# The load phase of a two-layer encoder kernel: squares held behind the splits of x, first weights in pieces, two chunks of x from ScalarE's queue

## The chip, the cores and the metric

The kernel runs on one core of a Trainium2 chip. The metric is the device time of one execution in microseconds; of several runs the median counts. All inputs start in the chip's memory (HBM), and the output ends there. Engines are named as in the profile: PE is TensorE, DVE VectorE, ACT ScalarE, POOL GpSimd, SP SyncE, which here only issues DMAs.

## What is computed

The reference is a trunk of two layers over 512 positions of width 1024, all float32. Each layer adds half of a SwiGLU feed-forward block, an attention mixer, half of a second feed-forward block, and a gated embedding. Cut to what the change touches:

```
h = x
h = h + 0.5 * swiglu(rmsnorm(h, norm_ffn1[0]), w_gate, w_up, w_down)
rmsnorm(x, g) = x * rsqrt(mean(x * x) + 1e-6) * g
swiglu(x)     = (silu(x @ w_gate) * (x @ w_up)) @ w_down
```

The first norm therefore needs the squares of all 1024 features of x, summed for each position. Its factor `rsqrt(...)` is one number for each position, so the kernel multiplies `x * g` by the weights first, and by that factor afterwards.

## The kernel before

**Layout.** The residual `h` is kept transposed, as 8 chunks (c = 0 to 7) of 128 features by 512 positions, 256 KB each. Weights come in units of 128 x 1024 (512 KB), eight 128 x 128 tiles side by side; a unit times the 8 chunks gives one output tile of 128 x 512.

**Three products for one.** To keep float32 accuracy each operand is split into a high part, rounded to the matmul's format, and a low part, the rest. ACT writes the high part (`activation` with Copy, L121 for weights, L168 for x times the gain), DVE the low part (L122 and L169), and PE does three matmuls (`mm3`, L142 high by high, L143 low x by high weights, L144 high x by low weights). One unit is 24 matmuls of 512 columns.

**The load phase.** `setup` loads the gains and the identity matrix from ACT's queue, makes a bfloat16 copy of the identity on DVE (`identb`, L97, read by nothing else in the program), and issues `WARM` = 12 matmuls on zeros (L109) to keep PE busy until data comes. Then it loads x chunk by chunk from SP's queue; after chunk 0 and chunk 2 it loads the first two weight units (`gu1[0, 0, 0]`, the gate, and `gu1[0, 0, 1]`, the up projection), which the first feed-forward tile takes from the list `ahead`. Each chunk is split as it lands (`norm_split`).

**The first norm.** `norm_square` (L175) squares a chunk on ACT; POOL adds the squares of chunks 1 to 7 into the tile `ssq` of chunk 0, seven adds in a row (L180), each of which needs the one before. `stat` then sums over the partitions with four small matmuls against ones on PE (L187, eight passes in the profile), DVE scales the sum (`ms`, L189), POOL takes the power -0.5 (`rcol`, L190), PE spreads the result over the partitions with four transposes (L206), and ACT copies it to `R` (L214). L236 and L238 multiply the finished output tiles by `R`.

**Order.** A tile framework schedules each engine's stream once, ahead of time, from the program's dependences and its own estimate of times; at run time every engine executes its stream in order and waits on semaphores. In the program `ffn` calls the eight `norm_square` behind the first two units (`if m == 0 and i == 0 and which == 1`); the scheduler moves squares forward to where it takes their chunk as landed. `keep_in_program_order`, used by the change, forbids that for one instruction: it stays behind everything traced before it on its engine.

**Buffers.** Raw weights have 3 buffers, high and low parts 4 each, temporaries (the squares of chunks 1 to 7 among them) 8; PE writes output tiles to 3 + 2 banks (`mm`, `sc`), so it can run some units ahead of `R`. Each DMA takes one of 8 semaphore lanes in turn, and a queue waits before it issues a DMA whose lane is still in use.

Of the kernel before, what the change touches and what calls it, by code (L numbers as in the profile page):

```python
# [11 lines left out]
BF16 = mybir.dt.bfloat16  # L12
AF = mybir.ActivationFunctionType
ALU = mybir.AluOpType

P = 128
# [12 lines left out]
UNIT = 8 * P  # L29
N_NORM = 4 * DEPTH + 1  # L30
OPEN = 2
PART = .8
WARM = 12
RPB_W = 48


class Trunk:
# [52 lines left out]
    def setup(self):  # L90
        nc, io = self.nc, self.io
        self.gain = self.cp.tile([P, N_NORM, KC], F32, name="gain")
        nc.scalar.dma_start(self.gain, io["gain"])
        self.ident = self.cp.tile([P, P], F32, name="ident")
        nc.scalar.dma_start(self.ident, io["ident"])
        self.identb = self.cp.tile([P, P], BF16, name="identb")
        nc.vector.tensor_copy(self.identb, self.ident)  # L97
        self.ones = self.cp.tile([P, P], F32, name="ones")
        nc.vector.memset(self.ones, 1.0)
        self.mhalf = self.cp.tile([P, 8], F32, name="mhalf")  # L100
        nc.vector.memset(self.mhalf, -0.5)

        warm = self.small("warm", [P, 1])
        nc.scalar.activation(warm, self.ones[:, 0:1], AF.Silu)
        idle = self.cp.tile([P, T], BF16, name="idle")
        nc.vector.memset(idle, 0.0)
        bank = self.tbank()
        for _ in range(WARM):
            nc.tensor.matmul(bank, idle[:, 0:P], idle, start=True, stop=True)  # L109
        self.h = [None] * KC  # L110
        self.begin_norm(0)
        for c in range(KC):
            self.h[c] = self.hp.tile([P, T], F32, tag="h", name=self.nm("h"))
            nc.sync.dma_start(self.h[c], io["xT"][:, c, :])
            self.norm_split(c)
            if c in (0, 2):
                self.ahead.append(self.unit(io["gu1"][0, 0, c // 2]))


    def split(self, src, hi, lo, lo_eng=None):  # L120
# [5 lines left out]
        self.turn = (self.turn + 1) % 3  # L126
        return self.nc.vector if self.turn else self.nc.gpsimd

    def unit(self, src, cols=UNIT, lo_eng=None):

        nc = self.nc
        raw = self.wr.tile([P, UNIT], F32, tag="wr", name=self.nm("wr"))
        hi = self.wh.tile([P, UNIT], F32R, tag="wh", name=self.nm("wh"))
        lo = self.wl.tile([P, UNIT], F32R, tag="wl", name=self.nm("wl"))
        nc.sync.dma_start(raw[:, :cols], src)
        self.split(raw[:, :cols], hi[:, :cols], lo[:, :cols], lo_eng)
        return hi, lo

    def mm3(self, out, stat, mov, start, stop):
# [32 lines left out]
    def norm_square(self, c):  # L172
        nc = self.nc
        sq = self.tmp() if c else self.small("ssq", [P, T], bufs=1)
        nc.scalar.activation(sq, self.h[c], AF.Square)  # L175
        if c == 0:
            self.acc = sq
        else:
            eng = nc.vector if c == KC - 1 and self.k else nc.gpsimd
            eng.tensor_tensor(self.acc, self.acc, sq, op=ALU.add)  # L180
# [881 lines left out]
```

## Time and profile before

| | us |
|---|---|
| median of 3 runs | 2126.43 |
| the three runs | 2123.27, 2126.43, 2127.14 |
| the profiled execution, its own time | 2126.64 |
| span of its instructions | 2124.8 |
| PE busy | 2085.4 (98%) |
| DVE busy | 1132.3 (53%) |
| ACT busy | 783.8 (37%) |
| POOL busy | 352.3 (17%) |

The span runs from the first to the last instruction; 1.84 us of the execution's time lie outside it. Start times in the rows below are microseconds from the start of the span. An engine's row in a timeline gives start, duration, engine, line, what it writes and reads, how many were merged, and in brackets how long the engine was idle before and what ended that. Durations of neighbours on one engine overlap a little, so the distance from one start to the next is what an instruction costs its engine. PE's granted clock, 1.00 or 0.50 in the rows, is its share of 2.4 GHz; 0.50 is 1.2 GHz.

### The profile page before, as it was taken

Reading aid. Unit: us, or ns where it says so; the run is one execution under the profiler, and the core shown is the slowest. Engines: PE = TensorE matmul, PEld = TensorE weight load, DVE = VectorE, ACT = ScalarE, POOL = GpSimd, SP = SyncE. Lnnn points to the kernel's source line nnn. Section 1 sums busy time; section 2 is a strip of 40 time slices with the busy share of each in tenths; the row PEclk is TensorE's granted clock in tenths of the full one; section 3 lists DMA queues with packets and bytes.
Section 4 is the critical chain, followed back from the end, with each engine's and each line's share of the span. In section 5 each row is a group of like instructions: output and inputs, shape, how many; then the busy total and the mean of one; then the engine's idle time right before and its main releaser. Section 6 shows DMA issues by size and latency. Waiting matters only on the chain.

```text
span 2124.8 us, 25520 instructions
## 1 busy us (share of the span) xinstructions
PE 2085.4 (98%) x9950; PEld 1734.6 (82%) x9950; DVE 1132.3 (53%) x1793; ACT 783.8 (37%) x1255; POOL 352.3 (17%) x248
## 2 busy tenths in 40 slices
PE   8999999999999999999999999999999999999998
PEld 6888888777787888888888888888888888888886
DVE  6554432699786444543354555333778744553334
ACT  4332222465544333222343233223656533232232
POOL 3111101233211111101111111013222210110111
PEclk9999999999999999999999999999999999999999
DMA  5333333221223233333333322334333223323331
GB/s 171 98 99 99 95 96 98 85 75 56 65 68 92 90 99 99 99 90 96 105 97 99 99 93 93 95 97 124 105 105 102 82 90 99 99 91 96 94 107 60
DMA packets 75385, 202.02 MB, mean 95 GB/s; under 512 B 16896, under 2 KB 24576, under 8 KB 75264
## 3 DMA queue, kind: packets, MB, share of 16 engines
q1 hardware_dynamic: 74976, 200.29, 30.8%
q8 instruction: 78, 1.28, 0.3%
q14 instruction: 43, 0.35, 0.1%
q10 hardware_dynamic: 288, 0.10, 0.0%
HBM read 191.97 MB, written 2.59 MB: 92 GB/s over the span
## 4 chain that ended last, share of the span: by engine, by line
PE 89%; DVE 5%; ACT 2%; issue 1%; POOL 1%; DMA 0%; SPq 0%; DVEq 0%; POOLq 0%; ACTq 0%
PE mm L143 15%; PE mm L144 15%; PE mm L142 15%; PE sc L142 12%; PE sc L143 12%; PE sc L144 12%; PE mm L322 1%; PE mm L323 1%; PE mm L324 1%; PE tr L349 1%; PE ob L359 1%; PE ob L360 1%; PE sc L428 1%; ACT wh L121 1%; DVE act L572 1%
## 5 line engine op out<-in xcount | busy, mean ns | idle before, releaser
L121 ACT ACTIVATE wh<-wr 128x1024 fp32r<-128x1024 f32 (+1 forms) x360 | 374.6, 1042 | 995.0 <-issue 431.1
L122 DVE TENSOR_TENSOR wl<-wr,wh 128x1024 fp32r<-128x1024 f32 (+1 forms) x343 | 510.2, 1488 | 314.1 <-ACT wh L121 313.1
L143 PE MATMUL mm<-act,wh 128*128 128x512 f32 (+1 forms) x1560 | 609.7, 391 | 3.0 <-DVE act L169 2.1
L142 PE MATMUL mm<-act,wh 128*128 128x512 f32 (+1 forms) x1560 | 609.1, 391 | 1.0 <-ACT wh L121 0.6
L144 PE MATMUL mm<-act,wl 128*128 128x512 f32 (+1 forms) x1560 | 608.3, 390 | 0.5 <-DVE wl L122 0.5
L144 PE MATMUL sc<-act,wl 128*128 128x512 f32 (+1 forms) x1138 | 442.5, 389 | 0.8 <-DVE wl L122 0.8
L142 PE MATMUL sc<-act,wh 128*128 128x512 f32 (+1 forms) x1138 | 442.9, 389 | 0.0
L143 PE MATMUL sc<-act,wh 128*128 128x512 f32 (+1 forms) x1138 | 442.5, 389 | 0.0
L143 PEld LDWEIGHTS mm<-act,wh 128*128 128x128 f32 x1560 | 293.4, 188 | 64.4 <-DVE act L169 5.3
L142 PEld LDWEIGHTS mm<-act,wh 128*128 128x128 f32 x1560 | 293.3, 188 | 60.0 <-ACT act L121 1.5
L144 PEld LDWEIGHTS mm<-act,wl 128*128 128x128 f32 x1560 | 293.2, 188 | 58.4 <-DVE wl L122 1.0
L239 POOL TENSOR_TENSOR tmp<-tmp,tmp 128x512 f32<-128x512 f32 x88 | 115.2, 1309 | 818.5 <-DVE tmp L238 783.7
L144 PEld LDWEIGHTS sc<-act,wl 128*128 128x128 f32 x1138 | 213.7, 188 | 45.1 <-DVE wl L122 1.2
L143 PEld LDWEIGHTS sc<-act,wh 128*128 128x128 f32 x1138 | 213.7, 188 | 44.1
L142 PEld LDWEIGHTS sc<-act,wh 128*128 128x128 f32 x1138 | 213.6, 188 | 43.8
L238 DVE TENSOR_TENSOR tmp<-sc,R 128x512 f32<-128x512 f32 x88 | 60.8, 691 | 276.8 <-PE sc L144 276.8
L180 POOL TENSOR_TENSOR ssq<-ssq,tmp 128x512 f32<-128x512 f32 x55 | 90.2, 1639 | 552.6 <-ACT tmp L175 525.7
L236 DVE TENSOR_TENSOR tmp<-mm,R 128x512 f32<-128x512 f32 x88 | 60.8, 691 | 130.4 <-PE mm L144 127.9
L121 ACT ACTIVATE act<-tmp 128x512 fp32r<-128x512 f32 x92 | 58.3, 634 | 117.3 <-POOL tmp L239 116.2
L322 PE MATMUL mm<-wh,act 128*128 128x256 f32 x256 | 74.4, 291 | 0.3 <-DVE act L337 0.3
L323 PE MATMUL mm<-wl,act 128*128 128x256 f32 x256 | 73.9, 289 | 0.0
L324 PE MATMUL mm<-wh,act 128*128 128x256 f32 x256 | 73.8, 288 | 0.0
(142 smaller groups left out, 1621.8 us busy)
## 6 DMA issues: line engine op xcount, KB each, us to landing
wr<-in_gu_dram SPq DMA_DIRECT2D x176, 512.0 KB, 3.5
wr<-in_dn_dram SPq DMA_DIRECT2D x64, 512.0 KB, 3.5
wr<-in_dn_dram SPq DMA_DIRECT2D x32, 384.0 KB, 3.1
wr<-in_qk_ab_dram SPq DMA_DIRECT2D x20, 512.0 KB, 3.5
wr<-in_plg_dram SPq DMA_DIRECT2D x16, 512.0 KB, 3.5
wr<-in_qk_c_dram SPq DMA_DIRECT2D x16, 512.0 KB, 3.7
act<-act SPq DMA_DIRECT2D x40, 128.0 KB, 2.2
wr<-in_v_ab_dram SPq DMA_DIRECT2D x8, 512.0 KB, 3.8
```

Of the source, the lines that this page charges most:

```text
L121: self.nc.scalar.activation(hi, src, AF.Copy)
L122: (lo_eng or self.nc.vector).tensor_tensor(lo, src, hi.bitcast(F32), op=ALU.subtract)
L142: mm(out, stat[0], mov[0], start=start, stop=False)
L143: mm(out, stat[0], mov[1], start=False, stop=False)
L144: mm(out, stat[1], mov[0], start=False, stop=stop)
L180: eng.tensor_tensor(self.acc, self.acc, sq, op=ALU.add)
L236: nc.vector.tensor_tensor(t1, pgu[0], R, op=ALU.mult)
L238: nc.vector.tensor_tensor(t2, pgu[1], R, op=ALU.mult)
L239: nc.gpsimd.tensor_tensor(t2, t1, t2, op=ALU.mult)
L322: nc.tensor.matmul(ps[b], xh, h, start=first, stop=False, skip_group_check=True)
L323: nc.tensor.matmul(ps[b], xh, l, start=False, stop=False, skip_group_check=True)
L324: nc.tensor.matmul(ps[b], xl, h, start=False, stop=last, skip_group_check=True)
```

## The change

- `WARM` goes from 12 to 11, and the bfloat16 identity is dropped. The identity itself is loaded from SP's queue behind the last chunk of x, no longer from ACT's queue ahead of everything.
- Chunks 1 and 3 of x are loaded from ACT's queue, the others from SP's as before.
- The first weight unit is loaded and split in four pieces of 256 columns, the second in two of 512.
- The square of chunk 0 in the first norm is pinned to its place in the program, behind everything traced earlier on ACT.

```
-WARM = 12
+WARM = 11
...
         self.ident = self.cp.tile([P, P], F32, name="ident")
-        nc.scalar.dma_start(self.ident, io["ident"])
-        self.identb = self.cp.tile([P, P], BF16, name="identb")
-        nc.vector.tensor_copy(self.identb, self.ident)
...
-            nc.sync.dma_start(self.h[c], io["xT"][:, c, :])
+            (nc.scalar if c in (1, 3) else nc.sync).dma_start(self.h[c], io["xT"][:, c, :])
             self.norm_split(c)
             if c in (0, 2):
-                self.ahead.append(self.unit(io["gu1"][0, 0, c // 2]))
+                self.ahead.append(self.unit(io["gu1"][0, 0, c // 2], pieces=4 - c))
+        nc.sync.dma_start(self.ident, io["ident"])
...
-    def unit(self, src, cols=UNIT, lo_eng=None):
+    def unit(self, src, cols=UNIT, lo_eng=None, pieces=1):
...
-        nc.sync.dma_start(raw[:, :cols], src)
-        self.split(raw[:, :cols], hi[:, :cols], lo[:, :cols], lo_eng)
+        n = cols // pieces
+        for x in (slice(i * n, i * n + n) for i in range(pieces)):
+            nc.sync.dma_start(raw[:, x], src[:, x])
+            self.split(raw[:, x], hi[:, x], lo[:, x], lo_eng)
...
-        nc.scalar.activation(sq, self.h[c], AF.Square)
+        ins = nc.scalar.activation(sq, self.h[c], AF.Square)
+        if c == 0 and self.k == 0:
+            self.tc.keep_in_program_order(ins)
```

How the streams move, at three places. Line numbers of the change are a few off those before: L119 and L120 are its weight splits (L121, L122 before), L189 and L208 its `stat` and transposes (L187, L206 before).

**ACT, the start of the load phase** (`act` is the high part of a chunk, `h` a chunk, `ssq` and `tmp` squares, `wh` and `wr` a weight unit's high part and raw form). Before:

```order
L168 ACTIVATE act_122<-h_120,gain 128x512
L175 ACTIVATE ssq_230<-h_120 128x512
L121 ACTIVATE wh_127<-wr_126 128x1024
L168 ACTIVATE act_134<-h_132,gain 128x512
L175 ACTIVATE tmp_232<-h_132 128x512
L175 ACTIVATE tmp_235<-h_138 128x512
L168 ACTIVATE act_140<-h_138,gain 128x512
```

With the change:

```order
L111 DMA h_137<-in_xT_dram 128x512
L168 ACTIVATE act_118<-h_116,gain 128x512
L119 ACTIVATE wh_123<-wr_122 128x256 x2
L111 DMA h_158<-in_xT_dram 128x512
L119 ACTIVATE wh_123<-wr_122 128x256 x2
L168 ACTIVATE act_139<-h_137,gain 128x512
L175 ACTIVATE tmp_241<-h_137 128x512
```

The square of chunk 0 is gone from here, two loads of x are issued by ACT (the second between the pieces of the first unit), and the first unit's split stands as four pieces.

**ACT, the end of the load phase.** Before:

```order
L175 ACTIVATE tmp_247<-h_168 128x512
L168 ACTIVATE act_170<-h_168,gain 128x512
L175 ACTIVATE tmp_250<-h_174 128x512
L168 ACTIVATE act_176<-h_174,gain 128x512
L121 ACTIVATE wh_280<-wr_279 128x1024
L121 ACTIVATE wh_311<-wr_310 128x1024
```

With the change:

```order
L168 ACTIVATE act_178<-h_176,gain 128x512
L175 ACTIVATE tmp_253<-h_170 128x512
L168 ACTIVATE act_184<-h_182,gain 128x512
L175 ACTIVATE ssq_239<-h_116 128x512
L175 ACTIVATE tmp_256<-h_176 128x512
L175 ACTIVATE tmp_259<-h_182 128x512
L119 ACTIVATE wh_289<-wr_288 128x1024
```

The square of chunk 0 (`ssq`) now stands behind the last chunk's split, with the last two squares behind it; before, the squares went between the splits, chunk 0's first. `ssq` is the tile into which POOL adds the others, so its seven adds, whose order is unchanged, now all come behind this instruction.

**PE, around the sum of squares** (`mm` and `sc` are output tiles, `sc` here the second unit's; `tr` is the sum or the transposes). Before:

```order
L143 MATMUL sc_205<-act_177,wh_145 128x512
L144 MATMUL sc_205<-act_176,wl_146 128x512
L187 MATMUL tr_254<-ones,ssq_230 128x1 x4
L142 MATMUL mm_285<-act_122,wh_280 128x512
L143 MATMUL mm_285<-act_123,wh_280 128x512
L144 MATMUL mm_285<-act_122,wl_281 128x512
L142 MATMUL mm_285<-act_134,wh_280 128x512
L143 MATMUL mm_285<-act_135,wh_280 128x512
L206 MATMUL tr_263<-ident,rcol_260 128x128 x4
```

With the change:

```order
L143 MATMUL sc_214<-act_185,wh_150 128x512
L144 MATMUL sc_214<-act_184,wl_151 128x512
L142 MATMUL mm_294<-act_118,wh_289 128x512
L143 MATMUL mm_294<-act_119,wh_289 128x512
L144 MATMUL mm_294<-act_118,wl_290 128x512
L189 MATMUL tr_263<-ones,ssq_239 128x1 x4
L142 MATMUL mm_294<-act_139,wh_289 128x512
L143 MATMUL mm_294<-act_140,wh_289 128x512
L144 MATMUL mm_294<-act_139,wl_290 128x512
L142 MATMUL mm_294<-act_145,wh_289 128x512
L208 MATMUL tr_272<-ident,rcol_269 128x128 x4
```

The four matmuls that read `ssq` come three matmuls later in the stream, the transposes two later: 53 matmuls of the three products stand ahead of the transposes before, 55 with the change. On DVE the scaling `ms` of the sum now stands ahead of the fifth unit's weight split, before it stood behind. Behind the first norm the streams of PE, DVE, ACT and POOL are the same; on SP some of the small loads of a later table stand at other places between the weight units.

## Rows read from the trace of the kernel before

**Rows 1.** The page's first part: busy time, share of the span, instructions.
```profile
PE 2085.4 (98%) x9950; PEld 1734.6 (82%) x9950; DVE 1132.3 (53%) x1793; ACT 783.8 (37%) x1255; POOL 352.3 (17%) x248
```
**Rows 2.** The timeline of PE, load phase.
```profile
1.34 4.89 PE L109 MATMUL tr<-idle 128*128 128x512 bf16 x12 [1.34 <-DVE idle L106]
...
6.87 0.50 PE L142 MATMUL mm<-act,wh 128*128 128x512 f32 x1 [0.65 <-ACT wh L121]
...
21.20 0.50 PE L143 MATMUL mm<-act,wh 128*128 128x512 f32 x1 [0.27 <-DVE act L169]
```
**Rows 3.** The chain that ended last, around the first norm: start, us, what.
```profile
24.01 0.23 PE sc L144
24.24 0.80 PE tr L187 x8
...
25.07 0.17 DVE ms L189
...
25.31 1.03 POOL rcol L190
...
26.39 0.65 PE tr L206 x4
```
**Rows 4.** The timeline of DVE, 0 to 42 us.
```profile
5.97 0.23 DVE L97 CAST identb<-ident 128x128 bf16<-128x128 f32 x1 [4.70 <-DMA ident<-in_ident_dram]
...
12.59 8.56 DVE L169 SCALAR_TENSOR_TENSOR act<-h,gain,act 128x512 fp32r<-128x512 f32 x5
...
28.91 1.21 DVE L122 TENSOR_TENSOR wl<-wr,wh 128x1024 fp32r<-128x1024 f32 x1
...
37.77 2.29 DVE L122 TENSOR_TENSOR wl<-wr,wh 128x1024 fp32r<-128x1024 f32 x1 [0.23 <-ACT wh L121]
```
**Rows 5.** The timeline of POOL, 0 to 40 us, and one add from 286 us.
```profile
11.75 8.85 POOL L180 TENSOR_TENSOR ssq<-ssq,tmp 128x512 f32<-128x512 f32 x5 [0.16 <-ACT tmp L175]
...
29.22 2.05 POOL L239 TENSOR_TENSOR tmp<-tmp,tmp 128x512 f32<-128x512 f32 x1 [2.89 <-ACT tmp L237]
37.69 1.29 POOL L239 TENSOR_TENSOR tmp<-tmp,tmp 128x512 f32<-128x512 f32 x1 [6.42 <-DVE tmp L238]
...
286.47 1.30 POOL L180 TENSOR_TENSOR ssq<-ssq,tmp 128x512 f32<-128x512 f32 x1 [29.86 <-ACT tmp L175]
```
**Rows 6.** The timeline of ACT and its DMA queue, load phase.
```profile
0.73 0.40 ACTq L93 DMA_DIRECT2D gain<-in_gain_dram  x1
...
4.51 0.72 ACT L168 ACTIVATE act<-h,gain 128x512 fp32r<-128x512 f32 x1 [1.36 <-DMA gain<-in_gain_dram]
...
5.76 1.06 ACT L121 ACTIVATE wh<-wr 128x1024 fp32r<-128x1024 f32 x1
6.73 0.71 ACT L168 ACTIVATE act<-h,gain 128x512 fp32r<-128x512 f32 x1
...
12.03 0.71 ACT L168 ACTIVATE act<-h,gain 128x512 fp32r<-128x512 f32 x1
12.65 0.61 ACT L175 ACTIVATE tmp<-h 128x512 f32<-128x512 f32 x1
13.17 0.71 ACT L168 ACTIVATE act<-h,gain 128x512 fp32r<-128x512 f32 x1
...
16.05 1.99 ACT L121 ACTIVATE wh<-wr 128x1024 fp32r<-128x1024 f32 x2
```
**Rows 7.** DMA issues (KB, us to landing): gain, identity, then chunk 3 of x.
```profile
gain<-in_gain_dram ACTq DMA_DIRECT2D x1, 36.0 KB, 3.8
ident<-in_ident_dram ACTq DMA_DIRECT2D x1, 64.0 KB, 4.8
...
h<-in_xT_dram SPq DMA_DIRECT2D x1, 256.0 KB, 7.0
```
**Rows 8.** PE's timeline after a long idle stretch, and windows of it with PEclk.
```profile
395.27 1.44 PE L428 MATMUL sc<-act,act 128*128 128x256 f32 x4 [2.54 <-DVE act L270]
...
395.00:396.00 1.00, 0.73 (x3) 0.73 (x4) 0.90 (x2) 0.00 (x0) 0.00 (x0) 0.50 0.00 0
...
398.00:399.00 1.00, 1.00 (x9) 1.00 (x9) 0.91 (x3) 0.00 (x0) 0.00 (x0) 0.89 0.00 0
```

## The prediction

> **What bounds the kernel now.** I read the page's busy shares first: PE is busy 98% of the span [rows 1], so a change of the load phase counts only by how much earlier or later PE gets through it; all behind it shifts along. The next view is PE's timeline. The reader sees warm-up matmuls until 1.34 + 4.89 = 6.23, the first real matmul at 6.87, released by ACT's weight split, and at 21.20 still a wait for DVE's low part of the last chunk of x [rows 2]. From there the chain of waits is solid: the second unit's last matmul at 24.01, the sum of squares at 24.24, DVE's scaling at 25.07, POOL's power at 25.31, the transposes at 26.39, which end at 26.39 + 0.65 = 27.04 [rows 3]. That end is my mark: 53 matmuls of the three products stand ahead of it, 55 with the change, so the fair mark for before is 27.04 + 2 x 0.23 = 27.5.
>
> Why PE starves until 21.20 is seen on DVE and POOL. Five low parts of x take DVE 8.56, 1.71 each [rows 4], while POOL's five adds beside them take 8.85, 1.77 each [rows 5]; an add alone takes 1.30 [rows 5]. A weight split on DVE beside an add takes 2.29 instead of 1.21 [rows 4], so the two take turns. POOL is done at 11.75 + 8.85 = 20.60 [rows 5], before PE asks for the sum at 24.24: now the squares cost PE nothing as a wait of their own, but they slow DVE. ACT works nearly without a gap from 4.51 to 16.05 [rows 6].
>
> **The change part by part.**
>
> Small edits. The bfloat16 copy held DVE until the identity landed at 5.97 [rows 4]; dropped, it frees DVE a little earlier. One warm-up less ends them 0.41 (4.89 / 12) sooner, at 5.82 [rows 2]. The first piece of weights is one quarter of a split that takes ACT 6.73 - 5.76 = 0.97 [rows 6], so PE can start about 1 us before its 6.87 [rows 2]. The identity moves on SP behind the last chunk of x, and SP's small loads shift; the identity is not needed before 27, and the loads stand before a weight unit that waits for a free raw buffer. DVE's scaling now stands ahead of the fifth unit's split; that unit is needed two units of 24 matmuls later, some 10 us, so I put it at nothing. All this helps PE only up to where it next waits, and the next paragraphs make that the sum of squares. So these edits count nothing at the end; if the sum were not awaited, the earlier start would show in full.
>
> Squares held: the gain. With the adds gone from beside them, DVE's low parts no longer alternate with POOL. ACT then sets the pace, a chunk's split plus a square in 13.17 - 12.03 = 1.14 [rows 6]. PE has six matmuls (1.4) for each chunk, so it finishes the two units a little behind ACT's last chunk, at about 19, not 24.24: some 5 us ahead.
>
> Squares held: the price. POOL's first add needs the square of chunk 0, now behind all eight splits of x on ACT. When is it done? Before, ACT did eight splits of x, eight squares and two weight splits from 4.51 to 16.05 [rows 6]. Up to the end of chunk 0's square it now does two squares fewer, at 13.17 - 12.65 = 0.52 each [rows 6]: 16.05 - 1.04 = 15.0. Six pieces instead of two whole splits are four more instructions. A 512-wide operation takes 0.61 and a 1024-wide one 1.06 [rows 6], so each has a fixed part of about 0.16, of which some overlaps; I take 0.1 each: 15.4, with 0.1 for the tail of the last one 15.5. Chunk 3's issue sits between the pieces; an issue takes ACT's queue 0.40 [rows 6], part of it under the running piece: 0 to 0.4, I take 0.2. Then the arrival of chunk 3: issued at about 5.8 (4.51, a split of 12.65 - 12.03 = 0.62 [rows 6], two pieces of some 0.32), wanted at about 9.4 (two more pieces, the issue, two splits and a square, both halves of the second unit). ACT's two loads of before landed after 3.8 and 4.8, chunk 3 from SP after 7.0 [rows 7]: arrival at 9.6, 10.6 or 12.8, a wait of 0.2, 1.2 or 3.4. I take 0.3, by the gain's 3.8, which like chunk 3 had no load ahead of it in ACT's queue. So chunk 0's square is there at 16.0, between 15.5 and 19.3.
>
> Here the Trainium skill speaks against the change: by "Trainium Kernel Development and Optimization", Key Constraints, loads issued from SP, ACT and POOL run on the same 16 DMA engines, and issuing from several "only saves the sequencer's issue time". By that chunk 3 would land no sooner than from SP, at 12.8, and the result would be the second case's below. The 3.8 and 4.8 are of small loads, so they do not refute it, but they are the only rows of that queue.
>
> Then seven adds. Two weight splits of DVE, of the third and fourth unit, fall among them. A split from 28.91 and the add behind it, done at 29.22 + 2.05 = 31.27 [rows 4, 5], make 2.36 for the pair. 5 x 1.30 + 2 x 2.36 = 11.2. Bounds: 7 x 1.30 = 9.1 alone, 7 x 1.77 = 12.4 at the pace of before [rows 5]. The sum is there at 27.2. PE, whose stream has only three matmuls of the third unit ahead of the sum, has long arrived: it stands idle from about 20 to 27, and everything of the program is queued behind it on PE. From the sum to the end of the transposes it took 27.04 - 24.24 = 2.8 [rows 3], plus 0.1 to load the squares: 30.1.
>
> PE's clock. After an idle stretch of 2.54 PE ran at a granted 0.50, 1.2 GHz, from 395.27 until some way into 398 to 399 (0.89) [rows 8]. Seven idle microseconds should do the same. About 2.9 us at half speed cost 1.45; some of it lies beside the wait for POOL's power, so I take 1.1, with 0 below and, if the slow stretch lasts twice as long, 2.9 above. Mark with the change: 31.2.
>
> Sum: 31.2 - 27.5 = +3.7 us. The 5 us that PE wins are lost in its wait for the adds, and a little more. The profiled execution took 2126.64 (span 2124.8 and 1.84 around it), so 2130.3; the median shown is 0.21 lower, so 2130.1. All low bounds give 15.5 + 9.1 + 2.9 = 27.5, no change; all high ones 19.3 + 12.4 + 2.9 + 2.9 = 37.5, +10.
>
> A measurement of this kernel tells about 0.2%, 4.3 us, from no change: 2122.2 to 2130.7 counts as the same.
>
> **The rivals.**
>
> Slower: chunk 3 comes late. It waits in ACT's stream behind two pieces of weights, and while ACT waits for it, the later splits and the square of chunk 0 wait too, microsecond for microsecond up to the mark. With SP's 7.0 [rows 7] the wait is 3.4, not 0.3: +6.8, 2133.2. It decides from a landing of 10.3 on (wait 0.9, +4.3). For it: the loads of the same stretch on SP; against: it is alone in its queue. 0.27.
>
> The same, by a short chain: adds near 9.1 to 10 and no loss of clock; then the gain and the price cancel: 0 to +1.5, about 2127. Against: the weight splits are ready just then, and 7 idle us are far more than 2.54. 0.15.
>
> Faster: PE keeps its head start of 5 us, 2121.4. That needs the last add by about 20, so that PE need not wait. Against: seven adds of 1.30 behind 15.5 cannot end before 24.6; only if the square of chunk 0 or the sum were elsewhere than the streams say. 0.04.
>
> That the pieces and the second queue do not bring the data earlier, so that PE starts no sooner, is not a case of its own: PE has 7 us of slack in front of the sum.
>
> **How the numbers follow.** The forecast, +3.7, has 0.54. It lies close under the bound of 0.2%, so I give 0.41 of it to the same and 0.13 to slower. With the rivals: slower 0.13 + 0.26 = 0.39, the same 0.41 + 0.01 + 0.15 = 0.57, faster 0.04. The range goes from 2125.6, the short chain's lower end less the spread of the runs, to 2133.6, just above the late chunk's 2133.2. The forecast's own range, within 2 us, is 2128.1 to 2132.1.
>
> **What would show it.** Right: the second unit's last matmul at 19 to 20, not 24; POOL's first add at about 16 and its last ending near 27; PE idle 6 to 8 us, put down to POOL's `ssq`; a granted clock of 0.50 behind it; DVE's low parts well below their 1.71; transposes ending at 30 to 32. Wrong: POOL's adds done by 23, or a sum of squares that PE does not wait for; ACT idle for more than 1 us before chunk 3's split would be the late chunk; a load phase as predicted and a total off by over 3 us would mean that a difference lies elsewhere.

## The result: slower by 0.40%, and the profile after

The change takes 2134.35 us, median of 6 runs (2132.84 to 2134.93); the kernel before, in the same comparison, 2125.80 (2123.27 to 2127.14). The ratio is 1.0040, 95% interval 1.0027 to 1.0053: 8.55 us slower, where +3.7 was forecast. The profiled execution took 2134.61, span 2132.8. PE is busy as long as before [rows 1] and only later, the page's first part says:

```profile
PE 2086.7 (98%) x9949; PEld 1736.2 (81%) x9949; DVE 1129.4 (53%) x1796; ACT 784.4 (37%) x1259; POOL 350.9 (16%) x248
```

ACT and its queue in the load phase, beside [rows 6]:

```profile
5.67 0.35 ACTq L111 DMA_DIRECT2D h<-in_xT_dram  x1
...
9.02 1.23 ACT L119 ACTIVATE wh<-wr 128x512 fp32r<-128x512 f32 x2 [0.47 <-DMA wr<-in_gu_dram]
12.25 0.72 ACT L168 ACTIVATE act<-h,gain 128x512 fp32r<-128x512 f32 x1 [2.00 <-DMA h<-in_xT_dram]
...
17.42 0.62 ACT L175 ACTIVATE ssq<-h 128x512 f32<-128x512 f32 x1
```

Two things are to be seen. The second load on ACT's queue, chunk 3, is issued at 5.67, and ACT stands 2.00 idle until it lands at 12.23; a weight piece cost another 0.47. And the square of chunk 0 (`ssq`) is done only at 17.42 + 0.62 = 18.04. DVE, beside [rows 4]:

```profile
15.27 0.75 DVE L169 SCALAR_TENSOR_TENSOR act<-h,gain,act 128x512 fp32r<-128x512 f32 x1 [0.38 <-ACT act L168]
...
31.21 0.16 DVE L191 TENSOR_SCALAR ms<-tr 128x4 f32<-128x4 f32 x1 [7.09 <-PE tr L189]
31.30 1.23 DVE L120 TENSOR_TENSOR wl<-wr,wh 128x1024 fp32r<-128x1024 f32 x1
```

Its low parts take 0.75, not 1.71: the gain is there. POOL, beside [rows 5]:

```profile
18.11 11.14 POOL L182 TENSOR_TENSOR ssq<-ssq,tmp 128x512 f32<-128x512 f32 x7 [17.68 <-ACT ssq L175]
31.45 1.95 POOL L192 TENSOR_TENSOR rcol<-ms,mhalf 128x4 f32<-128x4 f32 x1 [2.20 <-DVE ms L191]
```

The seven adds begin behind the square and end at 18.11 + 11.14 = 29.25; before, they ended at 20.60. The power takes 1.95, 1.03 before [rows 3], beside the weight split that DVE begins at 31.30. PE, beside [rows 2, 3]:

```profile
5.64 0.82 PE L142 MATMUL mm<-act,wh 128*128 128x512 f32 x1
...
21.04 0.39 PE L144 MATMUL sc<-act,wl 128*128 128x512 f32 x1
...
21.96 0.50 PE L144 MATMUL mm<-act,wl 128*128 128x512 f32 x1
29.31 1.87 PE L189 MATMUL tr<-ones,ssq 128*128 128x1 f32 x8 [6.85 <-POOL ssq L182]
...
33.46 1.11 PE L208 MATMUL tr<-ident,rcol 128*128 128x128 f32 x4 [0.37 <-POOL rcol L192]
...
55.74 0.39 PE L142 MATMUL mm<-act,wh 128*128 128x512 f32 x1
```

The same timeline of the kernel before has the second unit's last matmul here:

```profile
23.84 0.40 PE L144 MATMUL sc<-act,wl 128*128 128x512 f32 x1
```

With the change PE begins at 5.64, 1.2 us sooner than before, is through the first two units 2.8 sooner (their last matmul starts at 21.04, not 23.84), does three matmuls of the third unit, and then stands for 6.85 us, put down to POOL's `ssq`. The granted clock, 1.00 until 26, falls in that wait, seen in windows of the trace (stretch, its length, busy time and count of PE, PEld, DVE, ACT and POOL, then PEclk, DMA share, GB/s):

```profile
26.00:27.00 1.00, 0.00 (x0) 0.00 (x0) 0.00 (x0) 0.00 (x0) 0.92 (x2) 0.81 0.88 356
...
30.00:36.00 6.00, 5.63 (x18) 4.41 (x19) 2.07 (x4) 0.63 (x2) 1.95 (x1) 0.50 0.32 94
36.00:37.00 1.00, 1.00 (x4) 0.75 (x3) 0.53 (x1) 1.00 (x2) 0.33 (x1) 0.57 0.11 8
```

From some way into 26 to 27 until some way into 36 to 37 PE ran at 0.50, 1.2 GHz; from 37 on at 1.00 again. Last, the chain that ended last (start, us, what), which holds the story in order: chunk 3's load, the first of POOL's adds, the ones matmuls of the sum, then, behind power and transposes, matmuls at half clock and at full clock.

```profile
5.67 6.56 DMA h<-in_xT_dram
...
18.11 1.34 POOL ssq L182
...
29.31 1.88 PE tr L189 x8
...
34.57 0.43 PE mm L143
...
36.71 0.36 PE mm L142
37.29 0.23 PE mm L144
```

### The profile page after: what moved, and what is told of

It reads as the page before. It is cut to its first block, busy times and chain, and to the rows that moved or that the text cites. A ratio compares the mean times of both kernels' runs of the same rounds, so it can differ in the third digit from the quotient of the medians.

```text
span 2132.8 us, 25528 instructions
## 1 busy us (share of the span) xinstructions
PE 2086.7 (98%) x9949; PEld 1736.2 (81%) x9949; DVE 1129.4 (53%) x1796; ACT 784.4 (37%) x1259; POOL 350.9 (16%) x248
## 4 chain that ended last, share of the span: by engine, by line
PE 88%; DVE 5%; ACT 3%; POOL 1%; issue 1%; DMA 1%; SPq 0%; DVEq 0%; POOLq 0%; ACTq 0%
PE mm L143 15%; PE mm L144 15%; PE mm L142 15%; PE sc L142 12%; PE sc L143 12%; PE sc L144 12%; PE mm L324 1%; PE mm L325 1%; PE mm L326 1%; PE tr L351 1%; PE ob L361 1%; PE ob L362 1%; ACT wh L119 1%; PE sc L430 1%; DVE act L574 1%
## 5 line engine op out<-in xcount | busy, mean ns | idle before, releaser
L119 ACT ACTIVATE wh<-wr 128x1024 fp32r<-128x1024 f32 (+1 forms) x364 | 375.2, 1032 | 992.9 <-issue 434.3
L120 DVE TENSOR_TENSOR wl<-wr,wh 128x1024 fp32r<-128x1024 f32 (+2 forms) x347 | 512.0, 1477 | 316.8 <-ACT wh L119 315.7
L119 ACT ACTIVATE act<-tmp 128x512 fp32r<-128x512 f32 x92 | 58.3, 634 | 115.6 <-POOL tmp L241 114.8
```

Source lines behind the costliest of these rows:

```text
L119: self.nc.scalar.activation(hi, src, AF.Copy)
L120: (lo_eng or self.nc.vector).tensor_tensor(lo, src, hi.bitcast(F32), op=ALU.subtract)
```

## The experiments

Three theories stood against each other. **W**: the loss is PE's wait for adds that can't start before the held square, and the half clock that the wait brings. **D**: it is the late landing of the chunk that ACT's queue loads. **P**: it is the pieces of the first weights, with the later identity load. One place in PE's timeline measures the load phase in every trace: the start of the seventh unit, with 144 product matmuls ahead of it. The units next to it take 5.44 each in every trace. The table has it beside the medians (differences are to the kernel before of the same comparison, whose medians were 2125.80 to 2126.68).

| kernel | seventh unit | to before | median | to before | ratio, 95% interval |
|---|---|---|---|---|---|
| before | 47.54 | | | | |
| the change | 55.74 | +8.20 | 2134.35 | +8.55 | 1.0040 (1.0027 to 1.0053) |
| e1: change without the pin | 52.09 | +4.55 | 2130.27 | +4.21 | 1.0021 (1.0012 to 1.0030) |
| e2: change, all of x on SP | 53.92 | +6.38 | 2132.92 | +6.86 | 1.0031 (1.0019 to 1.0042) |
| e3: before with the pin | 54.28 | +6.74 | 2132.66 | +6.60 | 1.0031 (1.0019 to 1.0042) |
| e4: change, sum later | 48.17 | +0.63 | 2127.17 | +1.11 | 1.0006 (0.9998 to 1.0015) |
| e5: change, PE kept busy | 56.91 | +9.37 | 2136.80 | +10.25 | 1.0049 (1.0036 to 1.0062) |
| e6: pieces alone | 48.97 | +1.43 | 2128.30 | +1.75 | 1.0009 (1.0000 to 1.0018) |
| e7: before, pin, sum and transposes later | 43.57 | -3.97 | 2122.29 | -4.26 | 0.9980 (0.9971 to 0.9989) |
| e8: as e7, with the pieces | 44.78 | -2.76 | 2123.76 | -2.79 | 0.9986 (0.9977 to 0.9995) |
| e9: change, chunk 3 on SP | 53.14 | +5.60 | 2131.58 | +5.25 | 1.0025 (1.0015 to 1.0035) |
| e10: as e7, chunk 1 on ACT | 44.06 | -3.48 | 2123.06 | -3.27 | 0.9986 (0.9977 to 0.9995) |
| e11: as e7, without the pin | 47.43 | -0.11 | 2126.35 | -0.33 | 0.9998 (0.9989 to 1.0007) |
| e12: e3, PE kept busy | 53.11 | +5.57 | 2132.56 | +5.88 | 1.0028 (1.0018 to 1.0037) |

The two columns of differences agree within 0.9 us in every row, and the change's traced execution is 7.97 longer than that of the kernel before, so the change's loss lies ahead of the seventh unit.

A seventh unit in the table is that of one execution, and one execution scatters. The kernels e3, e7 and e12 have the same streams up to the third unit, and it starts at 20.77, 20.40 and 19.51: in e3 chunk 2 landed late, in e7 the clock fell for a while, in e12 neither. So differences under some 1.3 us between two rows are not to be read as effects of an edit unless something else in the traces shows them. Behind the seventh unit executions differ as well: between 540 and 580 us the granted clock was 0.87 in the trace of the kernel before and 1.00 in that of e10, whose 2119.52 is the lowest of its 11 runs.

**e3, the pin alone.** The kernel before with only this:

```
-        nc.scalar.activation(sq, self.h[c], AF.Square)
+        ins = nc.scalar.activation(sq, self.h[c], AF.Square)
+        if c == 0 and self.k == 0:
+            self.tc.keep_in_program_order(ins)
```

> The kernel before with the pin alone: loads, pieces and warm-up as before. Theory W: chunk 0's square ends near 16, the adds near 27.4, PE waits some 6 us and falls to half clock, the total is 2130 to 2132, so at least half of the loss of the change comes with this one line. Rivals D and P: 2125 to 2127, as before.

Measured +6.60, a little above W's range and far from the others'. Its PE timeline:

```profile
20.77 0.39 PE L142 MATMUL mm<-act,wh 128*128 128x512 f32 x1
...
29.47 1.87 PE L189 MATMUL tr<-ones,ssq 128*128 128x1 f32 x8 [7.86 <-POOL ssq L182]
```

The third unit starts at 20.77, and the wait for `ssq` is 7.86. So most of the loss needs neither the second queue nor the pieces. ACT's timeline of this run also shows something that I had wrong:

```profile
5.83 1.06 ACT L121 ACTIVATE wh<-wr 128x1024 fp32r<-128x1024 f32 x1 [0.54 <-DMA wr<-in_gu_dram]
...
8.78 0.63 ACT L175 ACTIVATE tmp<-h 128x512 f32<-128x512 f32 x1 [0.76 <-DMA h<-in_xT_dram]
...
16.72 0.62 ACT L175 ACTIVATE ssq<-h 128x512 f32<-128x512 f32 x1
17.24 2.94 ACT L121 ACTIVATE wh<-wr 128x1024 fp32r<-128x1024 f32 x3
```

ACT does the same work here as before, in another order, and comes to the next weights at 17.24 instead of 16.05 [rows 6]. The square that left the front left a gap of 0.54, in which ACT now waits for the first weights. The other part is no work of the pin: ACT stood 0.76 for chunk 2 here, 0.17 before, and with the same stream it comes to these weights at 16.64 in e7 and at 15.97 in e12.

**e1, the change without the pin.**

```
-        if c == 0 and self.k == 0:
-            self.tc.keep_in_program_order(ins)
```

> The change without its pin; the scheduler then puts chunk 0's square early on ACT and chunk 1's behind chunk 3's split. Theory W (PE's wait for the adds behind the held square, and the half clock after it, are the loss): the adds start near 13.5 instead of 18.1, end near 25.5 instead of 29.3, PE waits 2 to 3 us instead of 6.9 and keeps its clock, the total is 2126 to 2128. Rival D (chunk 3's late landing from ACT's queue is the loss): it is as late as with the change, so 2132 to 2134. Rival P (the pieces are the loss): 2132 to 2134.

Measured +4.21 (2130.27), between the ranges. PE's timeline and a window:

```profile
25.63 1.45 PE L187 MATMUL tr<-ones,ssq 128*128 128x1 f32 x8 [2.56 <-POOL ssq L180]
```
```profile
27.00:32.00 5.00, 5.00 (x15) 4.02 (x15) 1.52 (x3) 0.60 (x1) 1.95 (x1) 0.50 0.45 141
```

Without the pin the scheduler put chunk 1's square behind the split of chunk 3, so the late chunk held the adds: seven from 13.00 to 25.57, with DVE's low parts beside them. PE waited 2.56, as W had it, but did not keep its clock: the half clock followed, until some way into 32 to 33. So the pin is not the only way to be late with the squares; the second queue found another.

**e2 and e9, the second queue.** e2 loads all of x from SP, e9 all but chunk 1:

```
-            (nc.scalar if c in (1, 3) else nc.sync).dma_start(self.h[c], io["xT"][:, c, :])
+            nc.sync.dma_start(self.h[c], io["xT"][:, c, :])
```

```
+            (nc.scalar if c in (1,) else nc.sync).dma_start(self.h[c], io["xT"][:, c, :])
```

> The change with chunks 1 and 3 loaded from SP's queue again, pin and pieces kept. Theory W: the held square is done up to 2 us earlier, PE still waits 5 to 7 us for the adds and falls to half clock, so the total is 2131 to 2133. Rival D: ACT no longer waits 2 us for chunk 3 and the total returns to 2125 to 2127. Rival P: 2132 to 2134.

> The change with chunk 1 begun from ScalarE's queue and chunk 3 from the first queue as before the change. D (what the second queue costs is chunk 3's late issue, behind ScalarE's own work at 5.7): ScalarE's wait of 2.0 for chunk 3 is gone, the square of chunk 0 ends at 17 or earlier, 144th product matmul at 52 to 54 (change 55.7, both chunks on the first queue 53.9), total 2131 to 2133. Q (the second queue itself costs, by descriptors or by sharing the transfers' bandwidth): 144th product matmul at 55 or later, total 2134 or more.

e2 came out as W had it (2132.92, in P's range too): against the kernel before it is 1.7 us better than the change, by its seventh unit 1.82. e9 came out as D had it, 2.60 better than the change by the seventh unit. From ACT's queue chunk 1 came to its split 1.9 sooner (6.52 in e9, 8.40 in e2), and PE began the third unit at 19.26 instead of 21.83 (in e2 the clock was at 0.50 from 11 to 14, too); PE's wait for the adds leaves 0.8 of that by the seventh unit. ACT's square of chunk 0, POOL's row and chunk 1's DMA issue (KB, us to landing) in e9:

```profile
16.07 0.62 ACT L175 ACTIVATE ssq<-h 128x512 f32<-128x512 f32 x1
```
```profile
16.77 12.02 POOL L182 TENSOR_TENSOR ssq<-ssq,tmp 128x512 f32<-128x512 f32 x7 [16.33 <-ACT ssq L175]
30.99 1.02 POOL L192 TENSOR_TENSOR rcol<-ms,mhalf 128x4 f32<-128x4 f32 x1 [2.20 <-DVE ms L191]
```
```profile
h<-in_xT_dram ACTq DMA_DIRECT2D x1, 256.0 KB, 4.2
```

The square is done at 16.07 + 0.62 = 16.69, so chunk 3's lateness was worth 18.04 - 16.69 = 1.35 at this point. And the power takes 1.02: in this stream DVE's third weight split stands ahead of the sum, where it lengthens the adds (12.02) and not the power. So the 2.60 are not all chunk 3's: the last add ends only 0.46 sooner than with the change (28.79 against 29.25), the power takes 0.9 less, and the half clock ends sooner behind the sum, some way into 34 to 35.

**e6, the pieces alone** (the change with neither pin nor second queue; both edits as in e1 and e2).

> The change without the pin and with chunks 1 and 3 on the first queue again: what is left are the weight pieces, the later identity load and eleven warm-up matmuls. W (the pin is nearly all of the loss): the adds start near 13, the ones matmuls follow the second unit with under 2 us of idle, 144th product matmul at 46.5 to 48.5, total 2124.5 to 2127. P (the pieces or the identity cost by themselves): 144th product matmul at 49.5 or later, total 2128 to 2131.

Measured between: by the seventh unit nearer to W's 48.5 than to P's 49.5, by its median (+1.75) inside P's range. SP's queue and PE:

```profile
1.18 1.84 SPq L135 DMA_DIRECT2D wr<-in_gu_dram  x4
3.06 0.91 SPq L111 DMA_DIRECT2D h<-in_xT_dram  x2
```
```profile
8.90 0.77 PE L142 MATMUL mm<-act,wh 128*128 128x512 f32 x1 [2.20 <-ACT act L168]
...
27.83 0.65 PE L206 MATMUL tr<-ident,rcol 128*128 128x128 f32 x4 [1.02 <-POOL rcol L190]
```

Four pieces are four issues, 1.84 where the undivided load of before took one, 0.41, so chunk 1 is issued at 3.06 and not at 1.64 as before. PE starts at 5.60, runs out, and waits 2.20 for chunk 1. The early start is lost to the next chunk. But that is only 0.5 of the 1.43: the second unit's last matmul starts at 24.36, not 23.84. The other 0.9 comes behind it. Here too DVE's scaling stands ahead of a weight split, POOL's power takes 1.95, and PE waits 1.02 for it at 27.83; behind that wait the clock stays 1.00.

**e4, the sum behind the fourth unit** (the gating of the first tile put off accordingly).

```
-            nc.tensor.matmul(ps[:, i:i + 1], self.acc[:, x], self.ones[:, 0:1], start=True, stop=True)
+            ins = nc.tensor.matmul(ps[:, i:i + 1], self.acc[:, x], self.ones[:, 0:1], start=True, stop=True)
+            if self.k == 0:
+                self.tc.keep_in_program_order(ins)
```

> The change with the sum of squares, and with it the first tile's gating, moved behind the fourth weight unit on PE (its matmuls pinned there), so that PE has two more units of 24 matmuls to do while POOL adds. Theory W: no wait for the adds and no fall of the clock; PE has its 72 matmuls done about 3 us earlier than before, the total is 2121 to 2124. Rivals D and P, by which the loss is not that wait: 2131 to 2134.

The wait for the adds went, and the fifth unit began 3.2 us earlier than before (33.48 against 36.66). Still the total is that of the kernel before, outside both ranges. PE's timeline and a window:

```profile
35.90 1.12 PE L210 MATMUL tr<-ident,rcol 128*128 128x128 f32 x4 [1.71 <-POOL rcol L194]
```
```profile
36.00:38.00 2.00, 2.00 (x7) 1.81 (x8) 0.32 (x1) 0.60 (x1) 0.00 (x0) 0.50 0.74 116
```

Now the transposes wait 1.71 for the power, with only two matmuls between sum and transposes, and the clock falls again. One wait took the other's place.

**e7, e8, e10 and e11, the transposes later too.** e7 is the kernel before with the pin of e3, the sum of e4, the four transposes pinned behind 12 matmuls of the fifth unit, and the first two tiles' gating behind that unit. e8 is the same on e2 (pieces and later identity kept), e10 is e7 with chunk 1 on ACT's queue, e11 is e7 without the pin.

```
     def mm_unit(self, out, u, xs, start, stop, mid=None):
...
+            if mid and i == 4:
+                mid()
...
-                self.mm_unit(p, u, xg, True, True)
+                self.mm_unit(p, u, xg, True, True, (lambda: self.R) if first and m == 2 and j == 0 else None)
+                if first and m == 2 and j == 0:
+                    a += [self.gate(*x) for x in held]
```

> The kernel before with the pin, and with the sum pinned behind the fourth unit and the four transposes pinned into the middle of the fifth, the gating of the first two tiles put behind the fifth unit; nothing is left out. W (the pin is harmless and gives TensorE an earlier start once nothing on TensorE waits for what it delays): 96th product matmul at 31 to 33.5, no idle over 0.5 us and granted clock 1.00 up to 45, 144th at 43.5 to 45, total 2122 to 2123.5. If the wait only moves on to the gating or to the product tiles: 144th at 46 or later, total 2125 to 2128.

> The same late sum on the change with chunks 1 and 3 on the first queue again (pieces, later identity load, pin kept); nothing is left out. W: as the late sum on the kernel before, total 2122 to 2123.5, 144th product matmul at 44 to 45.5. If the pieces or the identity load matter by themselves once no wait covers them: apart from the late sum on the kernel before by 1 us or more.

> The late sum on the kernel before, with chunk 1 begun from ScalarE's queue; nothing is left out. D: chunk 1 is issued some 0.4 us sooner than from the first queue (1.24 against 1.64) and later chunks move up one place there, so the load phase gains 0 to 1 us: 144th product matmul at 42.5 to 43.6, total 2121 to 2122.5. Q: the gain is eaten by the late third transfer as in the change, total 2122.5 to 2124.

> The kernel before with the sum and the transposes later (as in the fastest kernel so far) but without the pin on chunk 0's square; nothing is left out. W (the pin gives TensorE its head start, the later sum only lets it keep it): the adds run beside the low parts of x again, those take 1.71 each, the second unit ends near 24 as before, 144th product matmul at 46.3 to 47.3, total 2125 to 2126.5. If the later sum is the whole gain: 144th product matmul at 43.5 to 44.5, total 2122 to 2123.5, as with the pin.

e7 does what W said but for one point, and is faster than both kernels: 2122.29. The point is the clock, which was to be 1.00 up to 45: behind two waits in the load phase it was 0.50 from some way into 8 to 9 until some way into 11 to 12.

```profile
6.98 0.50 PE L142 MATMUL mm<-act,wh 128*128 128x512 f32 x1 [1.09 <-ACT wh L121]
...
8.24 0.66 PE L144 MATMUL mm<-act,wl 128*128 128x512 f32 x1 [0.52 <-DVE wl L122]
```

POOL and PE of e7, and a window of 25 us:

```profile
16.82 13.90 POOL L184 TENSOR_TENSOR ssq<-ssq,tmp 128x512 f32<-128x512 f32 x7 [16.38 <-ACT ssq L177]
32.51 1.95 POOL L196 TENSOR_TENSOR rcol<-ms,mhalf 128x4 f32<-128x4 f32 x1 [1.80 <-DVE ms L195]
```
```profile
31.29 0.95 PE L191 MATMUL tr<-ones,ssq 128*128 128x1 f32 x8
...
34.95 0.60 PE L212 MATMUL tr<-ident,rcol 128*128 128x128 f32 x4
```
```profile
20.00:45.00 25.00, 25.00 (x118) 20.82 (x117) 16.03 (x16) 8.74 (x11) 15.25 (x10) 1.00 0.59 159
```

The adds are later and longer than ever (16.82 + 13.90 = 30.72), and the power takes 1.95, but PE asks for them at 31.29 and 34.95, so neither costs anything; from 20 to 45 PE is busy throughout at 1.00. e8 begins its seventh unit 1.21 later than e7, and the medians are 1.5 apart, hardly more than the runs scatter; its trace shows where the time goes, PE waits 1.62 for chunk 1 behind the four pieces. e10 missed D's range by its seventh unit (44.06), and its median (2123.06) lies in Q's range, but does not differ measurably from e7's: chunk 1, issued from ACT at 1.72 behind gain and identity, not at 1.24, lets ACT go on only at 8.05 (6.83 in e7):

```profile
8.05 0.72 ACT L170 ACTIVATE act<-h,gain 128x512 fp32r<-128x512 f32 x1 [1.32 <-DMA h<-in_xT_dram]
```

e11 came out as W had it but for a few tenths (47.43, expected up to 47.3): the kernel before, within what can be told. The later sum alone wins nothing; PE gets to it no sooner, since the adds run beside DVE's low parts again, as POOL's timeline shows:

```profile
12.62 8.17 POOL L182 TENSOR_TENSOR ssq<-ssq,tmp 128x512 f32<-128x512 f32 x5 [1.46 <-ACT tmp L177]
```

**e5 and e12, the wait filled.** e5 is the change with 34 matmuls on zeros on PE ahead of the sum:

```
+            for _ in range(34):
+                self.tc.keep_in_program_order(
+                    nc.tensor.matmul(fill, self.idle[:, 0:P], self.idle, start=True, stop=True))
```

> The change, with 34 added matmuls of 512 zero columns on TensorE between the second unit and the ones matmuls of the sum; nothing is left out. They are some 7 us of work with no reader, so TensorE waits for the adds in all but name, yet does not idle. W (the wait alone costs, the clock is incidental): the ones matmuls start near 29.4 as in the change, the 144th product matmul starts at 55.7 and the total is 2133 to 2135. C (the half clock after the idle costs some 2.5 us of its own): granted clock 1.00 from 26 to 37, ones matmuls and transposes 0.8 and 0.7 instead of 1.87 and 1.11, 144th product matmul at 52.5 to 53.7, total 2131 to 2132.5.

Both missed: it is 10.25 above the kernel before, where the change is 8.55 above it. The three matmuls of the third unit moved behind the fill, DVE's third weight split moved beside the adds, which took 12.94, and behind the sum PE had short gaps, after which the clock fell anyway, from about 34 to some way into 37 to 38. PE and a window:

```profile
31.08 1.05 PE L194 MATMUL tr<-ones,ssq 128*128 128x1 f32 x8 [0.90 <-POOL ssq L182]
...
33.49 0.65 PE L215 MATMUL tr<-ident,rcol 128*128 128x128 f32 x4 [0.79 <-POOL rcol L199]
```
```profile
35.00:36.00 1.00, 1.00 (x3) 0.78 (x3) 1.00 (x2) 0.46 (x1) 0.00 (x0) 0.50 0.31 29
```

So e12 took the simplest kernel with the wait, e3, kept those three matmuls ahead of the same fill, and filled the gap between sum and transposes too, with 7 more.

> The kernel before with the pin, and with matmuls on zeros that keep TensorE busy in its wait: 34 behind the third matmul of the third unit, ahead of the sum, and 7 between the sum and the transposes, with the first tile's gating behind the third unit; nothing is left out. Against the pin alone (144th product matmul at 54.3) the four matmuls that stood between sum and transposes come behind them, 0.9 later. C (the half clock has a price of its own, behind the sum): granted clock 1.00 up to 40, ones matmuls 0.8 to 1.05, transposes 0.65, 144th product matmul at 52.9 to 53.7, total 2131 to 2132. If the half clock costs nothing, or goes on all the same: 144th product matmul at 54.3 to 55.3, total 2132.5 to 2134.

PE's timeline of e12, and a window of 10 us:

```profile
20.42 7.29 PE L228 MATMUL tr<-idle 128*128 128x512 bf16 x33
29.09 1.05 PE L191 MATMUL tr<-ones,ssq 128*128 128x1 f32 x8 [1.39 <-POOL ssq L184]
...
31.52 0.64 PE L212 MATMUL tr<-ident,rcol 128*128 128x128 f32 x4
```
```profile
30.00:40.00 10.00, 10.00 (x49) 7.69 (x49) 4.06 (x6) 3.44 (x5) 2.32 (x2) 1.00 0.17 14
```

The fill shows as 33 of its 34 matmuls. The clock stayed at 1.00, and the seventh unit starts at 53.11, where C had it. The median, 2132.56, does not decide: it is just above C's range and just inside the rival's, and e3's is 2132.66. From the last add, 16.15 + 12.89 = 29.04, to the fourth unit at 36.79 it is 7.75; in e3 from 17.41 + 12.00 = 29.41 to 37.96 it is 8.55. With the four matmuls that e12 has to do behind the transposes (0.9) the half clock cost e3 0.80 + 0.9 = 1.7, by one trace of each. By these it is a price of its own, and a smaller one than the wait.

## Why the prediction was wrong

The mechanism was right, two of its terms were too small, and one was counted as nothing.

| step | forecast | measured |
|---|---|---|
| DVE's low part | well below 1.71 | 0.75 |
| second unit's last matmul | 19 to 20 | 21.04 |
| square of chunk 0 done | 16.0 | 18.04 |
| seven adds | 11.2 | 11.14 |
| last add done | 27.2 | 29.25 |
| PE's wait | 6 to 8 | 6.85 |
| sum to end of transposes, but for the clock | 2.9 | 3.78 |
| half clock | 1.1 | 2.67 |
| all, to before | +3.7 | +8.2 |

**Right.** Holding the first square moves all seven adds behind it, since each needs the one before. DVE gains what it should, PE gets ahead, and then waits for POOL with the whole program behind it. The length of the adds was right almost to the tenth, though the 2.36 for a split and an add was read from a multiplication of output tiles (L239); in the change an add beside a split takes 2.14, one alone 1.3, and gaps of 0.07 make up the rest. That PE's wait came out as forecast is partly luck: both its ends came some 2 us late, the second unit (its head start was 2.8, not 5) and the last add, and chunk 3 stands ahead of both. With the pin alone and no such wait the third unit starts at 19.51 (e12). e7 and e11 show the wait as the cause, from the other side: the adds are there no earlier, and with nothing on PE waiting for them the pin's gain appears, -3.97 by the seventh unit against -0.11 without the pin. That is less than the rival of the kept head start (2121.4), and it needs the sum elsewhere, as that rival said.

**The square, 2.04 late.** Two steps failed. "I take 0.3, by the gain's 3.8": chunk 3 landed 12.23 - 5.67 = 6.56 after its issue, near SP's 7.0 [rows 7], and ACT waited 2.00. The row of the 36 KB gain was the wrong one to take, though not for its size or its queue alone: chunk 1, 256 KB from ACT's queue issued at 1.24, landed after 4.0. When chunk 3 was issued the DMA engines were full (DMA share 1.09 from 5 to 6, 0.29 from 1 to 2), and SP's load of x issued at 5.65 took 6.4. That this made it late was not tested by itself. The rule of the Trainium skill ("Trainium Kernel Development and Optimization", Key Constraints) that several issuing engines save issue time only had spoken for a late chunk 3; the trace agrees with it. With chunk 3 on SP the square came 1.35 sooner (e9). The rest, 16.69 against the forecast's 15.7 without the wait, I put down to "two squares fewer, at 13.17 - 12.65 = 0.52 each": work taken out of a stretch in which the engine waits for data saves nothing there. e3's gap of 0.54 shows that for the pin alone. In e9 ACT starts 0.11 later than before and waits 0.18 and 0.40 for weight pieces; the other 0.3 was not taken apart. The rival of the late chunk had this wait, and its 2133.2 is 1.2 below the median; but it is not the main cause, since the pin alone, without the second queue, costs 6.60.

**Sum to transposes, 0.9 long.** The change puts DVE's scaling ahead of the fifth unit's weight split. "I put it at nothing": I asked only whether the split would be late. The split had been ready while DVE stood for 7.09 in front of the scaling; it follows directly, at 31.30, and runs beside POOL's power at 31.45, which takes 1.95 instead of 1.03. In e2, e3 and e9, whose streams have that split ahead of the sum, the power takes 1.02 to 1.03. The step that failed is that one: DVE's place in the order was costed by who needs the split, and not by which engine runs beside it.

**Half clock, 1.6 short.** "About 2.9 us at half speed": it lasted some 10, from 26 to 37, and the part behind the sum alone 7.5. By rows of the chain: the ones matmuls 1.88 - 0.80 = 1.08, the transposes 1.11 - 0.65 = 0.46, and six matmuls behind them that take 2.51 instead of 6 x 0.23 = 1.38, 1.13. That is 2.67; my upper bound was 2.9. The four matmuls between sum and transposes cost nothing, since the power was awaited anyway. The size taken rested on one stretch [rows 8], and here the half clock lasted more than twice as long. e12 points to such a price in e3, 1.7, where the clock came back earlier, between 34 and 35.

These three give 2.05 + 0.9 + 1.6 = 4.5 on top of 3.7, the +8.2 of the seventh unit.

**Small edits.** They were to count nothing while PE has slack. On top of the pin that holds as far as can be told (e2 against e3: 6.38 and 6.74). "If the sum were not awaited, the earlier start would show in full": it does not, since PE waits for chunk 1 behind SP's four issues (2.20 in e6, 1.62 in e8), and the second unit ends 0.5 later than before (e6) and 1.2 later than in e7 (e8). I had costed the pieces on ACT and not on the queue that chunk 1 stands in.

**Open.** Parts don't add up, since each shifts the scheduler's streams: the pin costs 6.74 by itself and 8.20 - 4.55 = 3.65 on top of the rest. What makes the half clock last until 34 to 35 in e3 and until 36 to 37 in the change was not settled; it also fell sooner in e3, at 24, where PE's wait began sooner, and lasted some 10 us in both.

## What to carry to other kernels

An instruction at the head of a serial chain is moved with the whole chain: before holding it back, find the consumer at the other end and what is queued behind it, and move that consumer too, past enough work to cover each link (here sum and transposes both; moving one alone gave back all it won). Cutting a load into pieces, or giving it to another queue, is costed on the queue: what stands behind the added issues, and what the other engine does before it gets to issue. A wait of PE may have to be priced twice, once as idle time and once at half clock behind it. And one trace per kernel settles only differences larger than the scatter of traces with the same streams.

## What the runs showed of the hardware

- PE's clock fell after shorter idling than I had a row for, and stayed low for longer. An idle stretch of 1.02 left it at 1.00 (e6); one of 1.71 was followed by 0.50 for some 3 us (e4), one of 2.56 by over 6 us of it (e1). In e5 two gaps of 0.90 and 0.79, with others between, were followed by 0.50; in e12 one of 1.39 was not. Nor were the waits for chunk 3 of 1.68 in the change and 1.74 in e4, but in e7 waits of 1.09 and 0.52 were followed by 0.50 from 8 to 12. So the length of the last idle stretch does not tell by itself whether the clock falls, and the same streams (e3, e7, e12) fell in one execution and not in another.
- Among other loads a load of 256 KB took as long from ACT's queue (6.56, issued at 5.67) as from SP's (6.4, issued at 5.65); from ACT's queue at 1.24, with little under way, it took 4.0. The small loads at the start say nothing of the later ones.
- POOL's power on 128 x 4 numbers takes 1.02 to 1.03, and 1.95 wherever a weight split on DVE (two tiles read, fp32) began just ahead of it: 8 of the 14 traces, without exception. The Trainium skill ("SBUF — State Buffer", SBUF: two separate sides) has one port pair that a DVE instruction with two inputs in SBUF and a POOL instruction hold in turn, each for its whole length. The trace agrees: the operation of 512 numbers loses 0.93 to the split, an add of 128 x 512 beside such a split 0.8 (2.14 instead of 1.31).
